# Output projections that accumulate in a two-bank score tile instead of the attention's two result banks

## The chip, the cores and the metric

The kernel runs on one core of one Trainium2 chip, as one launch. The metric is the device time of a run in microseconds (us), smaller is better. TensorE (PE) does matrix products and transposes and writes them to PSUM; VectorE (DVE) and ScalarE (ACT) read PSUM; GpSimd (POOL) works from SBUF; SyncE (SP) issues the transfers. Each engine works through its own queue of instructions and waits there for semaphores of the others.

## The reference, cut to what matters

One decoder block on x of 1024 tokens by 1024 channels. A combined input projection feeds two head groups: native sparse attention (8 heads of width 64: a compressed, a selected and a windowed branch) and differential attention (4 heads, two softmax maps each, value width 128). The two groups are gated, joined and multiplied by `w_out`, and the residual is added.

```python
h = rms_norm(x, norm_g[layer]);  proj = h @ w_in[layer]
dq, dk, dv, dz, nq, nkv, nz, ng = jnp.split(proj, IN_SPLITS, axis=-1)
...
p = jax.nn.softmax(s, axis=-1)
p = p[:, :, 0] - lam * p[:, :, 1]                    # differential: two maps a head
o_diff = rms_norm(p @ v, diff_subln_g) * (1.0 - lam_init) * silu(dz)
...
o_nsa = (g[0] * o_cmp + g[1] * o_slc + g[2] * o_win) * silu(nz)
x = x + jnp.concatenate([o_diff, o_nsa], axis=-1) @ w_out[layer]
```

## The kernel before

Everything is float32; products with large operands are split into a high and a low part, so one product is three matmuls. There are three parts, one after the other.

Part one normalises x, projects it (lines L211 to L213) and parks queries, keys, values and gates in device memory. Part two does the sparse attention, for query tiles of 128 tokens from 0 to 7. Part three does the differential attention, for query tiles from 7 down to 0, so that its tiles see 1024, 896, 768, 640, 512, 384, 256 and 128 keys.

A differential query tile has four heads of two maps. Of each map, `softmax_pair` multiplies queries and keys into a score tile S (L465), DVE adds the position bias and finds the row's limit nm (L469), ACT takes the exponential and the row sum (L471). DVE makes the factor dc from the two sums (L774, L775). The second map is subtracted from the first: DVE does one part of the keys (L781), POOL the other (L778, L779). PE transposes the result in blocks of 128 (L786) into Tp, ACT or DVE copies Tp to SBUF (pT, L520 or L522), and PE multiplies it with the values into the result bank (L790). When the next tile's four heads have been written, `finish` transposes the gated result of the tile before (L155), makes its high part ch (ACT, L748) and low part cl (DVE, L749), and calls `out_proj`. In part two the same is done with 16 maps to a tile, POOL scales the probabilities (L618), and `out_proj` runs one tile late too (`pending`); the last tile's call stands after the loop, before part three.

`out_proj` makes 128 tokens by 1024 channels in two halves of 512: 12 matmuls each (L502 to L504), then one DVE addition of the residual (L505) and the store.

PSUM has eight banks of 512 floats a partition: pool psS holds two score tiles S of two banks each, psT two transposition banks Tp, psA two banks A. A holds the running result of the attention (O), the compressed scores, the gate transposes and the two halves of `out_proj`. S holds the scores. With up to 512 keys both maps of a head share one S tile; with more, each map takes one of its own.

What sets the order: the loops above are the order in which tiles are asked for, and a pool gives its buffers in that order. A scheduler with a model of time then orders each engine's instructions, and may move one up as far as its data and its buffer allow.

```python
psS = ctx.enter_context(tc.tile_pool(name="psS", bufs=2, space=PSUM))
psT = ctx.enter_context(tc.tile_pool(name="psT", bufs=2, space=PSUM))
psA = ctx.enter_context(tc.tile_pool(name="psA", bufs=2, space=PSUM))
```

Of the kernel before, what the change touches and what calls it, by code (L numbers as in the profile page):

```python
# [27 lines left out]
def block_kernel(ctx: ExitStack, tc: tile.TileContext, x, norm_g, w_in, dq_g, dk_g, lq1, lk1, lq2, lk2,  # L28
# [17 lines left out]
    def S_tile():  # L46
        return psS.tile([128, 1024], F32, tag="S", name="S")
# [4 lines left out]
    def A_tile():  # L52
        return psA.tile([128, 512], F32, tag="A", name="A")

# [112 lines left out]
    with ExitStack() as p1:  # L167
# [12 lines left out]
        def acc_tile():  # L180
            acc_n[0] += 1
            return A_tile() if acc_n[0] % 2 else S_tile()[:, :512]
# [23 lines left out]
        def mm_tokens(hi, lo, tt, n):  # L206
            A = acc_tile()
            t0 = 128 * tt
            for k in range(8):
                a, b = xh[:, k, t0:t0 + 128], xl[:, k, t0:t0 + 128]  # L210
                nc.tensor.matmul(A[:, :n], a, hi[:, k, :n], start=(k == 0), stop=False)  # L211
                nc.tensor.matmul(A[:, :n], a, lo[:, k, :n], start=False, stop=False)  # L212
                nc.tensor.matmul(A[:, :n], b, hi[:, k, :n], start=False, stop=(k == 7))  # L213
            return A

# [32 lines left out]
        with ExitStack() as pc:  # L248
# [5 lines left out]
            for tt in range(NT):  # L254
# [7 lines left out]
                A = mm_tokens(*w_c0, tt, 384)  # L262
# [42 lines left out]
        for tt in range(NT):  # L305
            A = mm_tokens(*w_c1, tt, 408)
# [81 lines left out]
        for th in range(2):  # L388
            for g in range(4):
                A = acc_tile()  # L390
# [19 lines left out]
        for tt in range(NT):  # L410
            A = mm_tokens(*w_dz, tt, 512)
# [81 lines left out]
        def out_proj(pool, ch, cl, wo, src, dst, xbufs):  # L493

            woh, wol = wo
            xt = pool.tile([128, 1024], F32, tag="xt", name="xt", bufs=xbufs)
            nc.sync.dma_start(xt, src)
            for nh in range(2):
                A = A_tile()
                c = slice(512 * nh, 512 * nh + 512)  # L500
                for k in range(4):
                    nc.tensor.matmul(A, ch[:, k], woh[:, k, c], start=(k == 0), stop=False)  # L502
                    nc.tensor.matmul(A, ch[:, k], wol[:, k, c], start=False, stop=False)  # L503
                    nc.tensor.matmul(A, cl[:, k], woh[:, k, c], start=False, stop=(k == 3))  # L504
                nc.vector.tensor_tensor(xt[:, c], A, xt[:, c], op=ALU.add)  # L505
                nc.sync.dma_start(dst[:, c], xt[:, c])
# [157 lines left out]
        for tt in range(NT):  # L664
# [5 lines left out]
            A = mm_tokens(*w_dv, tt, 512)  # L670
# [10 lines left out]
    with ExitStack() as p2:  # L681
# [9 lines left out]
        for qt in range(NT):  # L691
            t0 = 128 * qt
            QH, QL, nzt, gate, pg, rep = nxt
            Tp = A_tile()
            for g in range(4):
                nc.tensor.transpose(Tp[:, 128 * g:128 * g + 128], pg[:, g].rearrange("p k c -> p (k c)"), ident)
            pT = pT_tile("pcT")
            nc.scalar.activation(pT, Tp, AF.Copy)
            O = A_tile()
            nc.tensor.matmul(O, vcbd, pT, start=True, stop=False)  # L700
            if qt + 1 < NT:
                nxt = cmp_branch(qt + 1)


            for br in (1, 0):
                for gp in range(2):
                    Ps = early.pop((qt, br, gp), None) or nsa_softmax(qt, br, gp, QH, QL, gate, rep)
                    nsa_values(qt, br, gp, Ps, O)
            if pending:
                out_proj(*pending)  # L710
            nc.vector.tensor_tensor(nzt, O.rearrange("p (g q) -> p g q", g=4), nzt, op=ALU.mult)
            ch = st.tile([128, 4, 128], F32R, tag="ch", name="ch")
            cl = st.tile([128, 4, 128], F32R, tag="cl", name="cl")
            nc.scalar.activation(ch, nzt, AF.Copy)
            nc.gpsimd.tensor_tensor(cl, nzt, ch.bitcast(F32), op=ALU.subtract)
            pending = (st, ch, cl, wo_n, x[t0:t0 + 128], xa_d[qt], 1)
        O_first = A_tile()
        out_proj(*pending)

    nctx.close()  # L720


    with ExitStack() as p3:
# [20 lines left out]
        def finish(sq, qt):  # L744
            T3 = transposed(sq, 4)
            ch = st.tile([128, 4, 128], F32R, tag="ch", name="ch", bufs=2)
            cl = st.tile([128, 4, 128], F32R, tag="cl", name="cl", bufs=2)
            nc.scalar.activation(ch, T3, AF.Copy)  # L748
            nc.vector.tensor_tensor(cl, T3, ch.bitcast(F32), op=ALU.subtract)  # L749
            out_proj(st, ch, cl, wo_d, xa_d[qt], out[128 * qt:128 * qt + 128], 2)  # L750
# [4 lines left out]
        for i, qt in enumerate(order):  # L755
# [10 lines left out]
            for h in range(4):  # L766
# [6 lines left out]
                c = small.tile([128, 1], F32, tag="dc", name="dc")  # L773
# [58 lines left out]
```

## Time and profile before

| what | value |
|---|---|
| median of 3 runs | 808.14 us (807.63 to 808.69) |
| the profiled execution's own time | 807.29 us |
| its span, first to last instruction | 805.6 us |
| PE busy | 770.8 us, 96% of the span |
| DVE, ACT, POOL busy | 516.6, 356.6, 329.1 us |
| granted TensorE clock, mean | 0.996 of 2.4 GHz |

The profile is of one execution. Between its time and its span lie 1.7 us of start and end. Busy time of PE is that of pipelined matmuls with modelled ends: two that follow each other overlap. Part one lasts to about 380 us, part two to about 662 us, part three to the end.

### The profile page before, as it was taken

The numbers are of one execution on the slowest core, as the hardware profiler recorded it, in microseconds if no ns is written. First come the engines' busy times: TensorE is split into PE (matmuls) and PEld (weight loads), VectorE is DVE, ScalarE is ACT, GpSimd is POOL, SyncE is SP. The second block draws the span as 40 slices with busy tenths as digits, with TensorE's granted clock in tenths as the row PEclk, the third lists the DMA queues.
The fourth block names the chain that finished last, engine by engine and source line by source line (L and its number), as shares of the span: only waits on it lengthen the run. The fifth ranks groups of instructions, "written<-read, shape, count | busy, mean of one in ns | idle before, by whom it ended". The sixth has DMA issues, their size and how long they took to land. (4 is left out here: it accounts for less than half of the span.)

```text
span 805.6 us, 13024 instructions
## 1 busy us (share of the span) xinstructions
PE 770.8 (96%) x4457; PEld 640.9 (80%) x4457; DVE 516.6 (64%) x1239; ACT 356.6 (44%) x803; POOL 329.1 (41%) x393
## 2 busy tenths in 40 slices
PE   5999999999999999999979999999999999999997
PEld 4899988888888888888757778777777668998885
DVE  4643864488634548941487687786866287789843
ACT  6443322241323223101487557565647276766410
POOL 5816272250625526020256443443342227755321
PEclk9999999999999999999999999999999999999999
DMA  8538675472433545177494232341321815556233
GB/s 286 170 58 244 165 228 140 107 195 100 138 102 112 153 100 136 40 184 207 139 216 123 84 106 81 106 91 56 80 65 34 248 34 183 159 141 172 74 130 111
DMA packets 89297, 106.68 MB, mean 132 GB/s; under 512 B 15120, under 2 KB 62352, under 8 KB 89104
## 3 DMA queue, kind: packets, MB, share of 16 engines
q1 hardware_dynamic: 89232, 105.86, 47.4%
q8 instruction: 35, 0.57, 0.3%
q14 instruction: 30, 0.25, 0.1%
HBM read 72.27 MB, written 33.55 MB: 131 GB/s over the span
## 5 line engine op out<-in xcount | busy, mean ns | idle before, releaser
L471 ACT ACTIVATE P<-P,nm 128x128 f32<-128x128 f32 (+7 forms) x136 | 101.4, 748 | 42.6 <-DVE nm L469 39.0
L203 POOL TENSOR_TENSOR wlo<-raw,whi 128x512 fp32r<-128x512 f32 (+2 forms) x64 | 85.7, 1363 | 53.1 <-ACT whi L202 51.3
L522 ACT ACTIVATE pT<-Tp 128x512 f32<-128x512 f32 (+3 forms) x118 | 66.3, 573 | 72.9 <-PE Tp L649 60.4
L138 POOL TENSOR_TENSOR r<-ss,neghalf 128x8 f32<-128x8 f32 (+2 forms) x41 | 51.0, 1244 | 112.6 <-DVE ss L136 107.6
L211 PE MATMUL S<-whi,xh 128*128 128x512 f32 (+2 forms) x224 | 86.5, 386 | 0.6 <-ACT xh L244 0.6
L211 PE MATMUL A<-whi,xh 128*128 128x512 f32 (+2 forms) x224 | 86.8, 388 | 0.0
L213 PE MATMUL A<-whi,xl 128*128 128x512 f32 (+2 forms) x224 | 86.4, 386 | 0.0
L212 PE MATMUL S<-wlo,xh 128*128 128x512 f32 (+2 forms) x224 | 86.3, 385 | 0.0
L213 PE MATMUL S<-whi,xl 128*128 128x512 f32 (+2 forms) x224 | 86.0, 384 | 0.0
L212 PE MATMUL A<-wlo,xh 128*128 128x512 f32 (+2 forms) x224 | 85.6, 383 | 0.0
L618 POOL TENSOR_SCALAR P<-P,ssum 128x128 f32<-128x128 f32 (+7 forms) x72 | 52.2, 743 | 76.4 <-DVE ssum L614 44.2
L469 DVE CUSTOM_DVE_ANT_0 P<-S,D 128x128 f32<-128x128 f32 (+7 forms) x96 | 60.3, 661 | 22.7 <-PE S L465 14.1
L465 PE MATMUL S<-nsaK,QH 128*128 128x384 f32 (+2 forms) x192 | 68.2, 363 | 0.7 <-DVE nm L469 0.7
L654 PE MATMUL A<-pT,vsw 128*64 128x256 f32 x528 | 65.4, 386 | 2.0 <-ACT P L471 1.2
L465 PE MATMUL S<-nsaK,QL 128*128 128x384 f32 (+2 forms) x192 | 60.4, 329 | 0.0
L618 POOL TENSOR_SCALAR Pw<-Pw,ssum 128x640 f32<-128x640 f32 (+3 forms) x56 | 39.8, 730 | 47.7 <-DVE ssum L614 39.8
L163 DVE RECIPROCAL e<-e 128x512 f32<-128x512 f32 (+1 forms) x18 | 57.1, 3175 | 0.5
L520 DVE COPY pT<-Tp 128x512 f32<-128x512 f32 (+3 forms) x62 | 38.5, 620 | 28.3 <-PE Tp L649 28.2
L202 ACT ACTIVATE whi<-raw 128x512 fp32r<-128x512 f32 (+2 forms) x64 | 36.5, 606 | 44.1 <-DMA raw<-in_w_in_dram 38.1
L654 PEld LDWEIGHTS A<-pT,vsw 128*64 128x64 f32 x528 | 34.6, 136 | 25.3 <-ACT pT L522 2.7
L502 PE MATMUL A<-woh,ch 128*128 128x512 f32 x128 | 51.7, 404 | 1.9 <-ACT ch L748 1.5
L504 PE MATMUL A<-woh,cl 128*128 128x512 f32 x128 | 50.3, 395 | 0.1
(189 smaller groups left out, 1772.4 us busy)
## 6 DMA issues: line engine op xcount, KB each, us to landing
raw<-in_w_in_dram SPq DMA_DIRECT2D x48, 256.0 KB, 3.1
xt<-in_x_dram SPq DMA_DIRECT2D x16, 512.0 KB, 3.8
w<-in_cmp_w_dram SPq DMA_DIRECT2D x16, 256.0 KB, 3.8
QH<-nqs_d SPq DMA_DIRECT2D x16, 256.0 KB, 5.3
QL<-nqs_d SPq DMA_DIRECT2D x16, 256.0 KB, 6.6
xa_d<-xt SPq DMA_DIRECT2D x16, 256.0 KB, 2.0
QH<-dqs_d SPq DMA_DIRECT2D x16, 256.0 KB, 5.3
QL<-dqs_d SPq DMA_DIRECT2D x16, 256.0 KB, 7.1
```

Source lines behind the costliest of these rows:

```text
L163: nc.vector.reciprocal(e, e)
L203: nc.gpsimd.tensor_tensor(l_, r_, h_.bitcast(F32), op=ALU.subtract)
L211: nc.tensor.matmul(A[:, :n], a, hi[:, k, :n], start=(k == 0), stop=False)
L212: nc.tensor.matmul(A[:, :n], a, lo[:, k, :n], start=False, stop=False)
L213: nc.tensor.matmul(A[:, :n], b, hi[:, k, :n], start=False, stop=(k == 7))
L465: nc.tensor.matmul(S[a][:, c0:c1], Q[:, heads[a]], Ks[a][:, w0 + c0 - o:w0 + c1 - o], start=Q is QH, stop=Q is QL)
L469: nc.vector.tensor_tensor_reduce(out=Ps[a][:, :n], in0=S[a][:, o:o + n], in1=biases[a], scale=-slopes[a], scalar=3e38, op0=ALU.add, op1=AL ...
L471: nc.scalar.activation(Ps[a][:, :n], Ps[a][:, :n], AF.Exp, scale=-1.0, bias=nm, accum_out=ssums[a])
L502: nc.tensor.matmul(A, ch[:, k], woh[:, k, c], start=(k == 0), stop=False)
L522: nc.scalar.activation(pT[:, :n], Tp[:, :n], AF.Copy)
L618: nc.gpsimd.tensor_scalar(P[:, :n], P[:, :n], ssum[:, g2, j:j + 1], 1.0, op0=ALU.mult, op1=ALU.mult)
L654: nc.tensor.matmul(O[64 * j:64 * j + 64, 256 * gp:256 * gp + 256], vsw[:, br, k0 + kt, 64 * j:64 * j + 64], pT[:, 256 * j:256 * j + 256], ...
```

## The change: the projection's halves lie in one score tile

`out_proj` asks for one score tile S, of two banks, and gives each half one of its banks; it asks for no A tile any more. Nothing else is edited, and the number of matmuls, additions and transfers is the same. Two lines are added, so what stood at L502 to L505 stands at L504 to L507 after the change, and every later line two further on.

```diff
             xt = pool.tile([128, 1024], F32, tag="xt", name="xt", bufs=xbufs)
             nc.sync.dma_start(xt, src)
+
+            S = S_tile()
             for nh in range(2):
-                A = A_tile()
                 c = slice(512 * nh, 512 * nh + 512)
+                A = S[:, c]
                 for k in range(4):
```

Since score tiles are given in the order in which they are asked for, the change moves PE's instructions. Three places follow; the numbers behind names are the program's own.

First, PE near the end of part two, before the change. A_6649 is the projection of the last but one tile of part two; S_6801 is the first score tile of part three (dkA holds keys of the differential heads).

```order
L649 MATMUL Tp_6301<-ident_72,Pw_6257 128x128
L502 MATMUL A_6649<-woh_3644,ch_6224 128x512
L503 MATMUL A_6649<-wol_3645,ch_6224 128x512
L465 MATMUL S_6801<-dkA_3629,QH_6782 128x512
L465 MATMUL S_6801<-dkA_3629,QL_6783 128x512
L465 MATMUL S_6801<-dkA_3629,QH_6782 128x512
L465 MATMUL S_6801<-dkA_3629,QL_6783 128x512
L504 MATMUL A_6649<-woh_3644,cl_6225 128x512
```

The scores of part three begin there 201 instructions ahead of the last value product of part two. Now the same of the changed kernel: A_6229 takes the last value products of part two, S_6680 is the projection of its last tile, S_6793 the first score tile of part three.

```order
L656 MATMUL A_6229<-pT_6624,vsw_3642 64x256 x2
L656 MATMUL A_6229<-pT_6617,vsw_3642 64x256 x2
L656 MATMUL A_6229<-pT_6610,vsw_3642 64x256 x2
L504 MATMUL S_6680<-woh_3644,ch_6673 128x512
L505 MATMUL S_6680<-wol_3645,ch_6673 128x512
L465 MATMUL S_6793<-dkA_3629,QH_6774 128x512
L465 MATMUL S_6793<-dkA_3629,QL_6775 128x512
```

The first scores of part three moved behind the last value product of part two and behind the start of its last projection.

Second, PE in part three around the query tile with 384 keys, before the change. S_7967 is that tile's last score tile (both maps of head 3); A_7438 is the projection of an earlier tile.

```order
L786 MATMUL Tp_7539<-ident_72,P_7515 128x128 x4
L465 MATMUL S_7967<-dkB_6739,QH_7688 128x384
L465 MATMUL S_7967<-dkB_6739,QL_7689 128x384
L465 MATMUL S_7967<-dkB_6739,QH_7688 128x384
L465 MATMUL S_7967<-dkB_6739,QL_7689 128x384
L502 MATMUL A_7438<-woh_6756,ch_7417 128x512
L503 MATMUL A_7438<-wol_6757,ch_7417 128x512
```

The transposes of the probabilities made from S_7967 stand 172 instructions behind it. In the changed kernel the same tile's last score tile is S_7955, its probabilities P2_7953, and S_7992 the projection of the tile before.

```order
L465 MATMUL S_7955<-dkB_6731,QH_7677 128x384
L465 MATMUL S_7955<-dkB_6731,QL_7678 128x384
L788 MATMUL Tp_7916<-ident_72,P_7897 128x128
L792 MATMUL A_7867<-dv_6730,pT_7920 128x128 x3
L788 MATMUL Tp_7944<-ident_72,P2_7925 128x128 x3
L788 MATMUL Tp_7972<-ident_72,P2_7953 128x128 x3
L792 MATMUL A_7867<-dv_6730,pT_7948 128x128 x3
L155 MATMUL Tp_7981<-ident_72,sq_7847 128x128 x4
L792 MATMUL A_7867<-dv_6730,pT_7976 128x128 x3
L504 MATMUL S_7992<-woh_6748,ch_7986 128x512
L505 MATMUL S_7992<-wol_6749,ch_7986 128x512
L465 MATMUL S_8045<-dkA_3629,QH_7859 128x256
```

Between the last scores and their transposes 7 instructions are left of 172, and the next tile's first scores (S_8045) stand behind the start of the projection S_7992.

## Rows read from the trace of the kernel before

**Rows 1.** The page: busy us of each engine, share of the span, instructions.

```profile
PE 770.8 (96%) x4457; PEld 640.9 (80%) x4457; DVE 516.6 (64%) x1239; ACT 356.6 (44%) x803; POOL 329.1 (41%) x393
```

**Rows 2.** Busy time by stretch: its length, then PE, PEld, DVE, ACT, POOL, granted clock.

```profile
420.00:645.00 225.00, 220.88 (x1490) 170.63 (x1488) 159.31 (x455) 133.75 (x290) 95.61 (x116) 1.00 0.36 98
645.00:690.20 45.20, 41.18 (x260) 33.63 (x261) 34.25 (x70) 30.85 (x57) 26.69 (x24) 0.96 0.44 132
690.20:763.00 72.80, 70.81 (x489) 64.83 (x489) 64.28 (x209) 44.90 (x119) 37.45 (x51) 1.00 0.47 125
763.00:783.00 20.00, 19.74 (x117) 16.13 (x116) 9.25 (x21) 3.62 (x8) 4.60 (x4) 1.00 0.38 131
```

**Rows 3.** Waits of PE from 645 to 802: us in total, times, longest.

```profile
PE S L465 <- DMA QL<-dqs_d: 2.5, 2, 1.4
...
PE S L465 <- DVE nm L469: 1.4, 1, 1.4
```

**Rows 4.** PE in order of time in part three: start, us, instruction.

```profile
709.57 0.39 PE L504 MATMUL A<-woh,cl 128*128 128x512 f32 x1
709.80 0.38 PE L786 MATMUL Tp<-ident,P 128*128 128x128 f32 x2
...
716.25 2.84 PE L790 MATMUL A<-dv,pT 128*128 128x128 f32 x24
718.92 0.38 PE L786 MATMUL Tp<-ident,P 128*128 128x128 f32 x2
```

**Rows 5.** Groups by line and shape, 645 to 802: count | busy us, mean ns.

```profile
L505 DVE TENSOR_TENSOR xt<-A,xt 128x512 f32<-128x512 f32 x18 | 12.4, 688 | 14.9 <-PE A L504 14.8
L471 ACT ACTIVATION_READ_ACCUMULATOR P<-P,nm 128x1 f32 x64 | 12.0, 187 | 0.0
L775 DVE TENSOR_SCALAR dc<-dc,dsum,neglam 128x1 f32<-128x1 f32 x32 | 8.6, 269 | 0.6
L469 DVE CUSTOM_DVE_ANT_0 P<-S,D 128x768 f32<-128x768 f32 x8 | 7.5, 952 | 4.1 <-PE S L465 4.1
L471 ACT ACTIVATE P<-P,nm 128x768 f32<-128x768 f32 x8 | 7.5, 933 | 5.2 <-DVE nm L469 5.0 <-DVE dc L774 0.2
L774 DVE RECIPROCAL dc<-dsum 128x1 f32<-128x1 f32 x32 | 5.0, 155 | 2.0 <-ACT P L471 2.0
L471 ACT ACTIVATE P<-P,nm 128x384 f32<-128x384 f32 x8 | 4.9, 611 | 3.8 <-DVE nm L469 3.8
L748 ACT ACTIVATE ch<-Tp 128x512 fp32r<-128x512 f32 x8 | 4.7, 589 | 20.1 <-PE Tp L155 20.1
L469 DVE CUSTOM_DVE_ANT_0 P<-S,D 128x384 f32<-128x384 f32 x8 | 4.2, 549 | 1.3 <-POOL P L779 0.8 <-PE S L465 0.5
L778 POOL TENSOR_SCALAR P<-P,dc 128x128 f32<-128x128 f32 x8 | 3.4, 425 | 5.0 <-DVE dc L775 4.6 <-ACT P L471 0.4
L781 DVE SCALAR_TENSOR_TENSOR P<-P,dc 128x384 f32<-128x384 f32 x4 | 3.3, 818 | 0.0
L779 POOL TENSOR_TENSOR P<-P,P 128x128 f32<-128x128 f32 x4 | 1.9, 482 | 0.3
L522 ACT ACTIVATE pT<-Tp 128x384 f32<-128x384 f32 x4 | 1.9, 483 | 2.2 <-PE Tp L786 2.2
L711 DVE TENSOR_TENSOR nzt<-A,nzt 128x512 f32<-128x512 f32 x1 | 0.7, 692 | 0.0
```

**Rows 6.** Busy time by stretch, as rows 2, around two pauses of PE.

```profile
400.00:420.00 20.00, 14.86 (x96) 11.01 (x97) 16.87 (x78) 14.91 (x46) 9.24 (x17) 1.00 1.01 234
682.00:686.70 4.70, 2.08 (x14) 1.48 (x13) 2.59 (x5) 4.70 (x10) 4.70 (x5) 1.00 1.03 268
686.80:690.20 3.40, 3.40 (x18) 3.30 (x17) 2.91 (x7) 2.16 (x5) 3.40 (x4) 0.50 1.06 308
```

**Rows 7.** Waits of PE from 420 to 645: us in total, times, longest.

```profile
PE A L696 <- DVE xt L505: 1.3, 2, 1.1
```

## The prediction

> **What bounds the kernel now.** The page comes first: PE is busy for 770.8 of 805.6 us, all other engines for 64% or less [rows 1]. So PE sets the time, and an edit that leaves PE's instructions as they are can only act through the moments at which PE waits. Where those lie is read from the stretches. In 420 to 645 (sparse attention) PE is idle for 225.00 - 220.88 = 4.1 us, in 645 to 690.2 (the passage into the differential part) for 45.20 - 41.18 = 4.0 us, in 690.2 to 783 for 1.99 + 0.26 = 2.25 us [rows 2]. The reader should see that the differential part runs nearly without a gap, although DVE is at 64.28 of 72.80 us (88%) in 690.2 to 763 and its work then falls to 9.25 of 20 us [rows 2]. That pair of rows shows how it is done: score tiles are made and softmaxed well ahead, and projections and value products, for which little DVE work is needed, fill PE meanwhile and at the end. The order says the same: in the 384-key tile 172 PE instructions lie between the last scores and their transposes.
>
> **What the change does.** The same 384 projection matmuls run (16 projections of 24), with the same additions and stores; nothing is added or removed on any engine. What moves is the row of buffers. Score tiles are given in the order in which they are asked for, and `out_proj` now stands in that order: the scores of tile i+1 are asked for behind the projection of tile i-1, whose transposes (L155) stand behind the heads of tile i. So the next tile's scores can't run ahead any more. Each tile becomes: projection with the first scores in it, the other scores, transposes and values, the next projection. PE works in order, so at the end of a tile it meets the softmax chain with little in hand.
>
> **A tile with 384 keys, step by step.** A matmul of 512 columns takes 0.23 us from start to start (709.57 to 709.80), a transpose or value product 0.111 us (2.67 us for 24) [rows 4]. A score tile of four 384-column matmuls is then 4 x 0.23 x 384/512 = 0.69 us. The chain from its end to a finished P is: two maps on DVE 2 x 0.549, one exponential 0.611 and its row sum 0.187, dc 0.155 + 0.269, POOL's block 0.425 + 0.482, together 3.23 us [rows 5]. In the new order, counted from the end of the tile's last scores (head 3), PE has one transpose and three value products (0.44 us), then needs head 2. Head 2's scores ended 0.69 us and five instructions (0.55 us) earlier, so its P is there at 3.23 - 1.24 = 1.99 us: PE waits 1.55 us. Its three transposes end at 2.32, head 3's P is there at 3.23: 0.9 us more. Then three transposes, three values, four transposes (L155) and three values reach 4.67 us; ch is ready 0.589 us after L155, at 4.92: 0.25 us. Sum 2.7 us for this tile, with no time for a semaphore between the steps.
>
> **The other tiles.** For 512, 256 and 128 keys the same count, with DVE and ACT times interpolated between the 384 and 768 rows (DVE 1.05 ns, ACT 0.84 ns a column, an estimate from rows 5), gives 2.1, 2.0 and 1.6 us. With 640 and 768 keys DVE paces the tile. For 768: eight maps 8 x 0.952, four times dc 4 x 0.42, four subtractions 4 x 0.818, five passes over 512 columns like L505 (5 x 0.688), about 1 us of copies: 17 us. PE has 24 x 0.23 for the projection, 8 x 0.69 for scores (512 + 256 columns, twice), 52 x 0.111 for transposes and values: 16.8 us. DVE and PE would be even, but no longer overlap at the tile's end, where an exponential and sum (1.12), dc (0.42), a subtraction (0.82) and a copy (about 0.58) stand in a row: I take 3.2 us of waiting each for 768 and 640 keys [rows 5]. Six tiles together: 3.2 + 3.2 + 2.1 + 2.7 + 2.0 + 1.6 = 14.8 us. What is there now in that stretch, 2.25 us, goes, among it the later of the two waits for QL (1.4 us) [rows 2, 3], since queries are now there long before they are used. Net +12.5. Bounds: at least one wait of 1 us a tile, 6 - 2.25 = +4, if the scheduler's spare work hides head 2's wait; at most 4 us a tile, 24 - 2.25 = +22, if semaphores and queues on DVE and ACT add half again.
>
> **The passage into part three.** The first scores used to run 201 instructions ahead of the last value product; now they stand behind the last projection's start. So PE first waits for O's gating on DVE (0.692) and ch on ACT (0.59): 1.3 us [rows 5]. Then the first head's chain of 1024 keys must fill. By the order its second map's scores end 12 projection matmuls and two score tiles after the start, 12 x 0.23 + 2 x 0.92 = 4.6 us; with the interpolated times (1.22 on DVE, 1.15 + 0.19 on ACT), dc 0.42 and POOL's 512 columns (0.9 for 128; 2.2 as an estimate for 512) P is there at 9.8 us, where PE has a projection and four score tiles, 5.5 + 3.7 = 9.2 us, to do: 0.6 us of waiting. ACT and POOL also convert the output weight there, in both kernels, so the 4.0 us that PE idles there now I leave as they are [rows 2], the wait for nm (1.4) and one for QL among them [rows 3]. Net +2, between 0 and +6.
>
> **Part two.** The two A banks are now free of the projection, so the waits of the gate transpose for the residual's addition end: -1.3 us [rows 7]. In exchange one of two score tiles is held for 5.5 us of matmuls and an addition of 0.69 in each of eight tiles. The order there leaves some 30 to 110 PE instructions between scores and their transposes, thin in the first three tiles alone. I take +1.3, so 0 net, between -4 (all idle time of rows 2's first stretch goes) and +6.
>
> **The sum.** 807.29 us of the profiled execution + 12.5 + 2 + 0 = 821.8; I say 822. The execution is 0.85 us below the median of 808.14, which is within the rounding of these estimates.
>
> **The clock, a rule against the change.** Twice the trace shows what a pause does to the granted clock. PE was busy 2.08 of 4.70 us in 682 to 686.7, and for the next 3.40 us the clock stood at 0.50, that is 1.2 GHz; but in 400 to 420, with 14.86 of 20 us busy, it stayed at 1.00, 2.4 GHz [rows 6]. So the short waits above are priced without a fall. The Trainium skill, "TensorE: Matmul & The Clock Gate", section "A second HAM failure mode: psum-queue depth-cycling", says that a kernel which cycles through PSUM banks and idles briefly between matmul groups can make the clock fall and rise again and again; by that rule, with the price that the trace gives a fall, the sum would be about 834. This trace bears out one fall of the two.
>
> **The rivals.** (a) The clock falls in each new pause: 3.40 us at half speed lose 1.7 us [rows 6]; seven pauses (six tiles and the passage) add 12: 834. Against it speaks the stretch from 400 to 420. (b) The waits are half as long, because DVE, freed from later tiles' maps, serves the current one sooner: 814. For it: DVE falls to 46% after 763 [rows 2]. Against it: the chain above has no queueing in it. (c) The waits are hidden: no more than what PE loses now, 808. It needs the scheduler's model to have filled each tile's end; the order shows 7 instructions there. (d) Faster: two separate banks let the halves follow each other while the first is added up, and O has a bank of its own beside the gate and compressed scores. The waits of 1.3 us [rows 7], the 2.5 us for QL [rows 3] and some more of the 4.1 us idle in part two [rows 2] go: 803. It decides if the tile's end costs under 0.5 us in each of eight tiles; 3.23 us of chain against 0.8 us of instructions in hand speak against it. The Trainium skill, "Perfetto Trace Analysis", section "Optimizing Tensor Performance", wants independent matmul groups to rotate through different PSUM banks so that one is drained under the next; that rule would have (d), and only the 1.3 us of rows 7 bear it out here. (e) Part two suffers too, as its DVE is at 159.31 of 225 us and has one score tile less during projections: +6 more, 828.
>
> **How the numbers follow.** Forecast 822 (818 to 826): 0.45. (b) 0.2, (e) 0.13, (a) 0.1, (c) 0.05, (d) 0.05, and 0.02 for slower than any. Faster by over 0.2% (about what a measurement can tell from no change) is (d), 0.05; the same is (c), 0.05; slower 0.9. The range from 811 to 832 leaves out (c), (d), (a) and the lower edge of (b).
>
> **What would show it.** In the new profile PE is idle for some 10 to 20 us more between the passage and 800 us, in pieces of 1 to 2 us, put down to POOL's L781 or DVE's L783 at the transposes L788, to copies pT at the values L792, and to ch at L504; DVE waits for scores at the tile's start. Waits of L698 for xt and of L465 for QL are gone. Part two takes the same time within 2 us. I am wrong if idle PE time is not in part three, if the granted clock falls below 0.98 in the mean, or if DVE, not PE, runs without gaps there.

## The result

| kernel | median (us) | lowest to highest | ratio to before, 95% interval |
|---|---|---|---|
| before | 807.88 | 806.07 to 808.69, 4 runs | 1 |
| changed | 838.39 | 836.33 to 842.12, 4 runs | 1.0386, 1.0345 to 1.0427 |

The change costs 30.5 us where 14 were forecast; 838 lies outside the range. The profiled execution took 842.12 us with a span of 840.4, so 34.8 us more than the span of before; it is the longest of the four, with a mean granted clock of 0.988 where the others have 0.990 to 0.993. First the page of the changed kernel, busy time by engine; it answers to [rows 1].

```profile
PE 785.8 (93%) x4457; PEld 645.2 (77%) x4457; DVE 518.9 (62%) x1239; ACT 359.1 (43%) x803; POOL 332.1 (40%) x393
```

The same 4457 instructions keep PE busy for 785.8 us in place of 770.8, and it is idle for 840.4 - 785.8 = 54.6 us in place of 34.8. So of the 34.8 us, 19.8 are idle time, and 15.0 are the same instructions taking longer. Only the first kind was in the forecast.

Where the idle time lies: the changed kernel's part three by stretches, each from the start of one projection to that of the next (columns as in [rows 2]). The first six hold the tiles with 768, 640, 512, 384, 256 and 128 keys.

```profile
707.40:732.50 25.10, 21.82 (x134) 18.06 (x133) 16.19 (x39) 11.85 (x25) 9.91 (x10) 1.00 0.34 95
732.50:753.90 21.40, 19.20 (x121) 16.52 (x121) 14.99 (x41) 10.19 (x22) 8.37 (x10) 1.00 0.39 111
753.90:771.90 18.00, 15.51 (x86) 12.22 (x85) 13.69 (x38) 8.46 (x20) 7.48 (x10) 1.00 0.47 132
771.90:789.70 17.80, 15.22 (x88) 12.51 (x88) 12.64 (x40) 7.29 (x20) 6.54 (x10) 1.00 0.44 120
789.70:806.20 16.50, 13.95 (x68) 11.10 (x69) 11.60 (x39) 6.23 (x20) 5.73 (x10) 0.89 0.29 95
806.20:820.30 14.10, 12.36 (x58) 9.90 (x57) 8.17 (x37) 5.27 (x20) 2.31 (x2) 0.86 0.27 93
820.30:829.60 9.30, 7.77 (x30) 5.74 (x29) 3.82 (x8) 1.19 (x2) 2.28 (x2) 0.86 0.08 30
```

Every stretch now has 1.5 to 3.3 us without PE work, where [rows 2] had 2.25 us in all for 690 to 783. The granted clock stays at 1.00 in four stretches and is below 0.9 in the last three. What PE waited for in 700 to 840, as in [rows 3] (us in total, times, longest):

```profile
PE A L792 <- DVE pT L522: 3.8, 4, 1.5
PE Tp L788 <- POOL P L781: 3.4, 7, 0.8
PE A L792 <- ACT pT L524: 3.4, 7, 0.6
PE S L504 <- DVE xt L507: 2.4, 5, 0.8
PE S L504 <- ACT ch L750: 1.5, 3, 0.7
PE Tp L788 <- DVE P L783: 1.0, 1, 1.0
```

The waits are those that the prediction listed, with one stranger: PE waits for the addition xt. That is the second half's first matmul, which waits for the first half's addition, though it writes another bank. Both halves are one tile, and the program seems to keep the dependence for the tile as a whole: in the run mixed below, whose halves are two tiles, the row is missing. The wait of the gate transposes [rows 7] is gone, as is that for QL [rows 3]. In part two, 420 to 640, one wait for a held score tile has taken its place:

```profile
PE S L465 <- DVE xt L507: 1.6, 1, 1.6
```

### The profile page after: what moved, and what is told of

The parts are those of the page before. It is cut to its first block, busy times and chain, and to the rows that moved or that the text cites. A ratio compares the mean times of both kernels' runs of the same rounds, so it can differ in the third digit from the quotient of the medians.

```text
span 840.4 us, 13034 instructions
## 1 busy us (share of the span) xinstructions
PE 785.8 (93%) x4457; PEld 645.2 (77%) x4457; DVE 518.9 (62%) x1239; ACT 359.1 (43%) x803; POOL 332.1 (40%) x393
## 4 chain that ended last, share of the span: by engine, by line
PE 75%; DVE 11%; DMA 4%; POOL 3%; issue 3%; ACT 2%; SPq 1%; POOLq 0%; DVEq 0%; ACTq 0%
PE S L465 8%; PE A L656 7%; PE Tp L651 7%; PE S L213 5%; PE S L212 5%; PE S L211 5%; PE A L211 5%; PE A L213 5%; PE A L212 5%; PE S L504 3%; DVE P L469 3%; PE S L506 3%; PE S L505 3%; PE A L792 3%; PE Tp L155 2%
## 5 line engine op out<-in xcount | busy, mean ns | idle before, releaser
L620 POOL TENSOR_SCALAR P<-P,ssum 128x128 f32<-128x128 f32 (+7 forms) x72 | 55.1, 787 | 56.5 <-DVE ssum L616 40.9
L504 PE MATMUL S<-woh,ch 128*128 128x512 f32 x128 | 53.8, 421 | 5.5 <-DVE xt L507 2.4
L506 PE MATMUL S<-woh,cl 128*128 128x512 f32 x128 | 51.4, 402 | 0.0
```

Of the source, the lines that this page charges most:

```text
L620: nc.gpsimd.tensor_scalar(P[:, :n], P[:, :n], ssum[:, g2, j:j + 1], 1.0, op0=ALU.mult, op1=ALU.mult)
```

## The experiments

Theory 1 is the prediction's: the projection stands in the row of score tiles, so the next tile's scores can't run ahead, and each tile's end lies open. Rival 1: the wait between the halves, in all 16 projections, does most of it. Rival 2: part two suffers, and with it the clock. Rivals 3 and 4 came up later. All times are medians; a ratio is to runs of the kernel before on the same chip (medians 805.8 to 807.0 us there).

**s_two and s_three: where.** Part two's calls (the passage's too) have `xbufs` 1, part three's have 2, so one condition splits the change.

```diff
-            S = S_tile()
+            S = S_tile() if xbufs == 1 else None    # s_three: == 2
-                A = S[:, c]
+                A = S[:, c] if S is not None else A_tile()
```

> Score tile for the eight projections of part two (the passage's among them), A banks again for the eight of part three. Theory 1 (the row of score tiles lays each differential tile's end open): 810 to 816, the loss that is left is the passage and some of part two. Rival 1 (the two halves are one tile, so the second half waits for the addition of the first, in all 16 projections): about half of the loss stays, 820 to 825. Rival 2 (part two has too few score tiles, and its pauses lower the clock): 825 or more.

> A banks for the eight projections of part two, score tile for the eight of part three. Theory 1: 830 to 837, nearly the whole loss. Rival 1: about half, 820 to 825. Rival 2: 808 to 815.

Measured: s_two 810.66 us, 1.0042 (1.0027 to 1.0057); s_three 831.68 us, 1.0295 (1.0273 to 1.0318). So some 24 us come from part three's eight projections and 3 to 4 from the other eight; Rival 2 falls, and Rival 1, which needs about equal halves.

s_three is also the kernel in which the loss can be taken apart, since from 690 us to the end it has as many PE instructions as the kernel before: first before, then s_three, columns as above.

```profile
690.00:805.60 115.60, 107.83 (x683) 94.29 (x682) 81.48 (x243) 50.66 (x133) 45.83 (x58) 1.00 0.42 123
```

```profile
690.00:834.00 144.00, 122.95 (x683) 101.14 (x681) 86.59 (x246) 53.98 (x135) 48.06 (x60) 0.95 0.34 100
```

28.4 us more: 21.05 - 7.77 = 13.3 are idle, 15.1 are longer busy time for 683 instructions as before. Of these, at most (1.00 - 0.95) x 144 = 7 us are the clock.

**adds_last: the wait between the halves.** All 24 matmuls first, then both additions.

```diff
-                nc.vector.tensor_tensor(xt[:, c], A, xt[:, c], op=ALU.add)
+            for nh in range(2):
+                c = slice(512 * nh, 512 * nh + 512)
+                nc.vector.tensor_tensor(xt[:, c], S[:, c], xt[:, c], op=ALU.add)
```

> The changed kernel, with the additions of both halves behind all 24 matmuls, so that the second half's matmuls cannot wait for the first half's addition. Theory 1: 832 to 836, since these waits are 3 to 5 us in the trace and the ends of the tiles stay open. Rival 1: 810 to 818. Rival 2: 836 to 840.

Measured: 849.35 us, 1.0524 (1.0507 to 1.0542): all three missed. The wait between the halves is gone, and the kernel is 11 us slower than the changed one. Of its waits in part three (line numbers 2 higher) one grew most, from 1.0 us:

```profile
PE Tp L790 <- DVE P L785: 7.3, 8, 1.8
```

The subtractions on DVE come later. That the score tile is given back later and DVE has two additions in a row would explain it; it was not tried apart. The run shows that the wait between the halves isn't what makes the change slow.

**early2: the row, a poor test.** `finish(*post)` is called ahead of head 2 of the next tile in place of behind head 3.

```diff
             for h in range(4):
+                if h == 2 and post:
+                    finish(*post)
...
-            if post:
-                finish(*post)
```

> The changed kernel, with the projection of tile i-1 asked for between heads 1 and 2 of tile i, and no longer behind head 3: the score tiles of the next tile's heads 0 and 1 then follow head 3's at once. Theory 1: 812 to 822, and PE's waits at L788 and L792 in part three (numbers of lines two higher there) fall to less than half. Rivals 1 and 2: 834 to 840, the waits for the first half's addition and those of part two stay.

Measured: 868.76 us, 1.0768 (1.0752 to 1.0784), above every range named. The edit put a new chain on the path, as its waits show:

```profile
PE Tp L155 <- POOL sq L808: 14.6, 7, 5.1
```

The gating of a tile (square, sums, power, product) used to have four heads of the next tile to hide behind, and now has two. The run says nothing on the row of score tiles.

**ring_only and ahead2: the row alone, and the held tile without it.** Rival 3 is that the projection holds one of two score tiles for some 6 us, so that all scores go through the other. ring_only is the kernel before, with a request for a score tile in the same place of the row, which one short matmul that nothing reads uses up.

```diff
+            if xbufs == 2:
+                nc.tensor.matmul(S_tile()[:, :128], ch[:, 0], woh[:, 0, :128], start=True, stop=True)
             for nh in range(2):
                 A = A_tile()
```

ahead2 is the changed kernel; the scores and softmaxes of one head are put into a function `maps`, and the next tile's heads 0 and 1 are asked for ahead of the projection.

```diff
+            if i + 1 < NT:
+                ahead = small.tile([128, 2, 4], F32, tag="dsum", name="dsum"), {}
+                for h in range(2):
+                    ahead[1][h] = maps(i + 1, nxt[0], nxt[1], ahead[0], h)
             if post:
                 finish(*post)
```

> The kernel before (halves in A banks), but in part three each projection also asks for a score tile, in the same place of the row, and writes one matmul of 128 columns into it, which nothing reads: the order of the row comes back, and the tile is held for 0.1 us in place of some 6. Theory 1 (the place in the row of score tiles decides): 822 to 829. Rival 3 (the projection holds one of the two score tiles while it runs and is added up, so that scores go through the other alone): 807 to 812.

> The changed kernel, with the scores and softmaxes of the next tile's heads 0 and 1 asked for ahead of the projection. The projection keeps its place behind the tile's last values, so the chain of gating is hidden again, and it still holds a score tile of two banks. Theory 1: 810 to 818, PE's waits at the transposes and values of part three fall to a third. Rival 3: 825 to 838, since one of two score tiles is held as before.

Measured: ring_only 814.56 us, 1.0091 (1.0055 to 1.0126); ahead2 818.44 us, 1.0137 (1.0101 to 1.0173). ahead2 lies just above Theory 1's range and takes back 20 of the 30 us, and PE's waits at the transposes and values of part three fall from 12.2 to 4.2 us, the third that was expected; so the row matters. ring_only lies in neither range, between the two: the row by itself costs 7 us of 24, so it isn't the whole cause.

**st_ahead2, a_ahead2 and ring_hold: each alone, and both.** Rival 4 is Rival 1 once more, for the 17 us between ring_only and s_three. st_ahead2 is s_three with ahead2's edit; a_ahead2 is the kernel before with it. ring_hold is ring_only with the tile held until the second half is added up; the halves lie in A banks, so the second needn't wait for the addition of the first.

```diff
+            if xbufs == 2:
+                H = S_tile()
+                nc.tensor.matmul(H[:, :128], ch[:, 0], woh[:, 0, :128], start=True, stop=True)
             for nh in range(2):
...
+            if xbufs == 2:
+                e = small.tile([128, 1], F32, tag="e", name="e")
+                nc.vector.tensor_tensor(e, H[:, :1], xt[:, 1023:], op=ALU.add)
```

> As the run in which the projection of part three only asks for a score tile, but the tile is now held until the second half is added up (a one-column operation that needs the second half's sum reads it); the halves still lie in A banks, so the second half never waits for the first half's addition. Two theories for the 17 us between order alone (814.6) and the score tile in part three (831.7). Theory 1b (order and holding together: the scores of the next tile must share the one tile that is left): 826 to 833. Rival 4 (the two halves are one tile for the semaphores, so the second half's matmuls wait for the first half's addition, and all behind them): 814 to 820.

> Score tile in part three alone, with the next tile's heads 0 and 1 asked for ahead of the projection: holding and the wait between the halves without the order. If order and holding cost much together only: 809 to 814, less than the order alone. If holding or the wait between halves costs by itself: 816 or more.

> The kernel before, halves in A banks, with the same two heads asked for ahead of the projection: neither order nor holding changes there, since the projection is in no row with the scores. 805 to 809 by both theories; a difference would show that the new place of the request does something of its own.

Measured: ring_hold 835.10 us, 1.0353 (1.0314 to 1.0392); st_ahead2 813.86 us, 1.0078 (1.0050 to 1.0106); a_ahead2 805.42 us, 0.9998 (0.9971 to 1.0024). st_ahead2 and a_ahead2 came out as expected, ring_hold 2 us above its range, far from Rival 4's. With these, part three's edits make a table of two causes (ratio to before):

| part three | scores of the next tile behind the projection | two heads of them ahead of it |
|---|---|---|
| no score tile held | 1.0091 (ring_only) | 0.9998 (a_ahead2) |
| score tile held | 1.0295 (s_three), 1.0353 (ring_hold) | 1.0078 (st_ahead2) |

Each alone costs 6 to 7 us, both together 24 to 28. In st_ahead2 heads 2 and 3 still stand behind the projection, so its 6 us are holding with a rest of the row. The wait between the halves isn't needed for the loss (in ring_hold PE waits 0.5 us in all for these additions at the projection): Rival 4 falls. What both together do is seen in PE's order of the 384-key tile. In ring_only, S_7975 is the last score tile, A_7852 the projection's second half, P2_7973 the last probabilities:

```
L465 MATMUL S_7975<-dkB_6739,QL_7695 128x384
L790 MATMUL Tp_7908<-ident_72,P_7889 128x128 x3
L506 MATMUL A_7852<-woh_6756,ch_7829 128x512
...
L508 MATMUL A_7852<-woh_6756,cl_7830 128x512
...
L790 MATMUL Tp_7992<-ident_72,P2_7973 128x128 x2
```

In ring_hold, with S_7983, A_7858 and P2_7981 in these places:

```
L509 MATMUL A_7858<-woh_6756,cl_7836 128x512
...
L465 MATMUL S_7955<-dkB_6739,QH_7700 128x384
...
L465 MATMUL S_7983<-dkB_6739,QL_7701 128x384
L798 MATMUL A_7895<-dv_6738,pT_7948 128x128 x3
L794 MATMUL Tp_7972<-ident_72,P2_7953 128x128 x3
L794 MATMUL Tp_8000<-ident_72,P2_7981 128x128 x2
```

Where the tile isn't held, all four heads' scores are written by the end of the first half, and the second half's twelve matmuls stand between them and their transposes. Where it is held, the scores trail through the one tile left, the projection runs out first, and the softmax chains of heads 2 and 3 follow with little beside them. The next pair tests whether this is all.

**mixed and mixed_late: half the holding, and twelve matmuls kept back.** mixed is s_three with only the first half in the score tile. mixed_late also makes `out_proj` a generator and asks for its second half behind the next tile's head 3.

```diff
+                A = S[:, c] if S is not None and nh == 0 else A_tile()
...
+                if h == 3 and rest:      # mixed_late
+                    list(rest)
```

> Part three alone, the first half in a score tile, the second in an A bank: no wait of the second half for the first half's addition, and the score tile is held for about half as long. Theory 1b: 819 to 826. Rival 4: 813 to 818.

> Part three, first half in a score tile and second half in an A bank, as in the run that came out at 833, but the second half's twelve matmuls are asked for behind the next tile's head 3 scores. The score tile is held as before; what changes is that twelve projection matmuls (2.8 us) are in hand when the last scores are written. If the loss is that the projection is used up while the scores of heads 2 and 3 wait for a score tile: 813 to 821. If holding the tile costs as such: 828 to 835.

Measured: mixed 832.97 us, 1.0334 (1.0296 to 1.0373); mixed_late 828.37 us, 1.0276 (1.0243 to 1.0310). Half the holding costs as much as all of it, a miss: the second half was put directly behind the first, ahead of the scores of heads 1 to 3. Keeping it back gains some 5 us at most (the intervals overlap, and part of it is the clock, 0.98 from 690 us on in mixed and 1.00 in mixed_late), not the 12 to 20 that were expected of it if the used-up projection were the whole loss; the time is at the lower edge of what was expected if holding the tile costs as such. PE's waits from 690 on, mixed:

```profile
PE Tp L788 <- DVE P L783: 6.3, 8, 1.4
...
PE Tp L788 <- POOL P L781: 2.3, 4, 1.1
PE A L792 <- ACT pT L524: 2.2, 4, 0.6
...
PE A L792 <- DVE pT L522: 0.7, 1, 0.7
```

and mixed_late (line numbers up to 5 higher):

```profile
PE A L797 <- ACT pT L525: 4.9, 8, 0.9
PE A L797 <- DVE pT L523: 2.7, 4, 0.9
...
PE Tp L793 <- DVE P L788: 2.0, 4, 0.7
```

The wait for finished probabilities falls from 8.6 to 2.0 us, so the matmuls kept back do hide the chain; but the waits of the value products for copies of the transposes rise from 2.9 to 7.6. So one step was covered, and PE waits at another instead.

**act_copies.** In part three `evac(Tp, 128 * kn, 10 ** 6)`: no copy on DVE.

> The changed kernel, with all copies of the transposes in part three on ScalarE, none on VectorE. If the copies that queue on VectorE behind maps and additions make up the part of the loss that was not foreseen: 832 to 836 (waits at L792 and L788 for copies of L522 are 5.7 us in the trace). If they only stand in for another wait that ends as late: 837 to 842.

Measured: 835.79 us, 1.0355 (1.0320 to 1.0390), which lies in the first range, but the changed kernel's interval overlaps it: inconclusive. The copies' waits move to ACT (row L792 from 3.4 to 5.9 us).

**pass_only.** The kernel before, with the score tile only in the call behind part two's loop (a flag around it).

> The kernel before, with only the last projection of part two, in the passage to part three, in a score tile. Theory 1: the passage costs 1.5 to 4 us, 809 to 811. If the 3 to 4 us lost with all eight projections of part two lie inside part two: 806.5 to 808.5.

Measured: 813.95 us, 1.0084 (1.0056 to 1.0112), above both ranges. Against s_two this is 3 us more, on another chip, with intervals that just meet. The traces agree better. The last matmul of part one (it starts later than the 380 us given above for the part's end) starts, by the number behind "to", in before, s_two and pass_only at

```profile
L213 PE MATMUL S<-whi,xl x224: 334/390/522, 17.5 to 392.6; 128*128 128x512 f32 x80, 128*128 128x384 f32 x16, 128*128 128x408 f32 x16
```

```profile
L213 PE MATMUL S<-whi,xl x224: 334/390/476, 17.4 to 391.3; 128*128 128x512 f32 x80, 128*128 128x384 f32 x16, 128*128 128x408 f32 x16
```

```profile
L213 PE MATMUL S<-whi,xl x224: 334/390/669, 17.4 to 393.4; 128*128 128x512 f32 x80, 128*128 128x384 f32 x16, 128*128 128x408 f32 x16
```

and their spans are 805.6, 808.9 and 811.0 us. Behind part one they take 413.0, 417.6 and 417.6 us. By these, seven more projections in score tiles change nothing, and the passage costs 4.6. Each is one execution, and falls of the clock behind part one differ between them by some 2 us (mean clock in 375 to 480: 1.00, 0.98, 0.98; in 655 to 706: 0.97, 0.97, 1.00), so the 4.6 is good to 2 us. The passage's waits in pass_only from 645 to 710 (line numbers of L781 and L792 2 higher):

```profile
PE Tp L790 <- POOL P L783: 2.0, 2, 1.6
PE S L504 <- ACT ch L716: 1.5, 1, 1.5
PE S L465 <- DVE nm L469: 1.4, 3, 0.6
```

## Why the prediction was wrong

**The place and the direction were right.** The loss is in part three and the passage, nothing in part two; the waits have the forecast's names, and the mean clock of 0.988 is above the 0.98 that would have spoken against it. The faster rival (d) had its gain (no wait for A) and lost far more.

**The step that failed is the price of the waits in the sum of the six tiles: +12.5, where part three measured +24 to +25.** It counted idle time alone, and as that it came out: in the first six stretches of the first section PE is idle for 3.28 + 2.20 + 2.49 + 2.58 + 2.55 + 1.74 = 14.84 us, where the forecast had 14.8, and s_three has 13.3 us more idle time than before. That the sums agree so closely is partly luck: the tile with 640 keys has 2.20 for 3.2, that with 256 has 2.55 for 2.0. One price in the working is also misread, that a value product takes 0.111 us. In the trace each is two matmuls:

```profile
L790 PE MATMUL A<-dv,pT 128*128 128x128 f32 x288 | 37.9, 281 | 0.5 <-ACT pT L522 0.5
L786 PE MATMUL Tp<-ident,P 128*128 128x128 f32 x144 | 22.7, 273 | 0.0
```

The loops ask for as many products as transposes, 144, so a product takes 0.22 us. With that the working for 384 keys gives 2.1 us of waiting in place of 2.7, and PE's work for 768 keys is 19.5 us in place of 16.8, more than DVE's 17.

What the forecast left out is what a wait costs beside its idle time. First, "the short waits above are priced without a fall". In the changed kernel, in the fifth stretch of the first section (columns as there):

```profile
798.00:800.00 2.00, 1.29 (x9) 1.06 (x9) 1.85 (x10) 1.71 (x7) 0.32 (x1) 1.00 0.80 225
800.00:802.00 2.00, 1.31 (x7) 0.89 (x7) 1.68 (x8) 0.59 (x4) 1.27 (x3) 1.00 0.21 55
802.00:804.00 2.00, 1.68 (x8) 1.49 (x8) 0.00 (x0) 0.38 (x1) 0.48 (x2) 0.62 0.71 244
804.00:806.00 2.00, 1.48 (x7) 1.08 (x7) 1.11 (x2) 0.60 (x1) 0.00 (x0) 0.50 0.00 0
```

PE is busy for 1.29 and 1.31 of 2 us, and the clock goes to 0.50, 1.2 GHz. By the stretches of the first section the last three tiles lose 0.11 x 16.5 + 0.14 x 14.1 + 0.14 x 9.3 = 5 us at most, s_three up to 7. This is rival (a), in two places rather than seven; the first four stretches wait as much at 1.00. The Trainium skill, "TensorE: Matmul & The Clock Gate", section "A second HAM failure mode: psum-queue depth-cycling", whose rule went with rival (a), tells of a kernel whose clock goes down and up again because PE idles briefly between groups of matmuls. The trace agrees in the last three stretches (0.86 to 0.89) and not in the four before them (1.00). mixed_late has 1.00 from 690 on and still loses 22 us, and of s_three's runs the one of 829.58 us has a mean clock of 0.995, as before has, and loses 22.7. So the clock is a part and no more.

Second, a wait costs more than its idle time, because matmuls overlap in a row and can't at a wait. PE in the 384-key tile of the changed kernel, in order of time, idle time before a row in brackets:

```profile
781.54 0.83 PE L792 MATMUL A<-dv,pT 128*128 128x128 f32 x6
...
782.92 0.27 PE L788 MATMUL Tp<-ident,P 128*128 128x128 f32 x1
784.69 0.94 PE L792 MATMUL A<-dv,pT 128*128 128x128 f32 x6 [1.50 <-DVE pT L522]
...
786.68 0.55 PE L788 MATMUL Tp<-ident,P 128*128 128x128 f32 x3 [0.51 <-POOL P L781]
```

From 782.92 to 784.69 are 1.77 us, where a transpose takes 0.111 in a row of them [rows 4]: 1.66 lost for 1.50 of idle time. The last transpose runs out alone, and its 0.27 us are booked as busy time. Behind the wait six matmuls take 0.94 us, where the six at 781.54, with no wait before them, take 0.83. mixed_late gives the price over many waits, since its clock stays at 1.00:

```profile
690.00:827.10 137.10, 117.40 (x692) 97.50 (x691) 86.97 (x249) 54.06 (x136) 48.73 (x61) 1.00 0.38 111
```

Against before it has 19.70 - 7.77 = 11.9 us more idle time and 117.40 - 107.83 = 9.6 us more busy time, of which nine more matmuls, at 0.111 to 0.23 us each, are 1 to 2. So about 8 us go with its 31 waits against 5 in before: an estimate of 0.3 us for each. The 30 waits of s_three are at that price 7.5 us more than the 5 of before. Idle time 13.3, clock up to 7, the edges of the waits 7.5: together 27.8 of the 28.4 us of s_three's profiled execution, the longest of its four.

**The tile with 384 keys** came to 2.7 us of waiting in the forecast and to 17.80 - 15.22 = 2.6 in the trace, by another path. The forecast gave the chains of heads 2 and 3 an idle DVE. DVE in that tile:

```profile
783.12 0.56 DVE L469 CUSTOM_DVE_ANT_0 P<-S,D 128x384 f32<-128x384 f32 x1 [0.42 <-PE S L465]
783.61 0.55 DVE L469 CUSTOM_DVE_ANT_0 P<-S,D 128x384 f32<-128x384 f32 x1
...
784.08 0.55 DVE L522 COPY pT<-Tp 128x384 f32<-128x384 f32 x1
```

Head 1's last transpose ends at 783.19, but the copy stands behind both maps of head 3 and starts at 784.08; PE waits 1.50 us for it, where the forecast had 1.55 us for head 2's chain. The agreement is luck in the place.

**"So the next tile's scores can't run ahead any more"** names half of the cause. The row alone costs 7 us; that the projection also holds one of two score tiles makes 24 of it. The prediction spoke of the held tile in part two only, where it cost one wait of 1.6 us, close to the +1.3 that it took.

**The passage, +2,** is 3.4 (s_two) to 7 us (pass_only), 4.6 by the traces: ch at 1.5 us as forecast (1.3), the first head's chain at 2 to 3 us rather than 0.6, as POOL's subtraction and the limits nm are waited for. Of the 4.0 us of waiting there before, which the forecast left as they were, those for QL are gone.

**Part two, 0,** holds within the 2 us of these traces: 417.6 us behind part one with and without it.

**The sum** with these terms is 807.3 + 13.3 idle + 7.5 for the edges of the waits + 4.6 for the passage = 833 without a fall of the clock, and 840 with 7 us of falls; 836 to 842 were measured. What stays open is why the row and the holding together make so many waits: 30 in s_three, where ring_only has 18 and st_ahead2 14, and before 5. The used-up projection is at most 5 us of it (mixed_late); what ends the rest of the waits as late was not tried apart.

## What to carry to other kernels

A buffer taken from the pool of the work that runs ahead cost twice here, by its place in the order and by being held, and both together cost more than the sum; try each alone. No version here beats the kernel before: with the halves in A banks the early request of two heads changes nothing (0.9998). When a bounding engine gets many short waits, price each at its idle time plus its edges (some 0.3 us here), count the instructions of a product in the trace before pricing it, and put some falls of the clock, at the price of the trace's own rows, into the likeliest case and not only into a rival.

## What was not expected of the hardware

In the fifth stretch of the first section the clock fell to 1.2 GHz behind two stretches with 1.29 and 1.31 us of work in 2. In the fourth it stayed at 1.00, 2.4 GHz, through three with less:

```profile
782.00:784.00 2.00, 1.20 (x9) 0.89 (x7) 1.58 (x7) 1.58 (x5) 0.00 (x0) 1.00 0.75 252
784.00:786.00 2.00, 1.18 (x8) 0.95 (x8) 1.92 (x10) 1.03 (x4) 0.73 (x2) 1.00 0.82 231
786.00:788.00 2.00, 1.15 (x9) 0.75 (x8) 0.38 (x2) 0.49 (x1) 1.43 (x3) 1.00 1.02 231
```

What made it fall in one place and not in the other stays open. And a wait of 1.50 us cost 1.66 by the starts of the instructions around it, with 0.11 more behind it.
